# A small product moved from the end of a three-block kernel to the two ends of its recurrence

## The chip, the cores and the metric

The kernel runs on one core of a Trainium2 chip. The time is that of one execution on the device, in microseconds (us), from the first to the last instruction with what lies around it; less is better. The engines are TensorE (PE in the profile; PEld is its weight load), VectorE (DVE), ScalarE (ACT), GpSimd (POOL) and SyncE (SP). Each takes its instructions from a queue of its own, in the order in which the program was built; ACTq, POOLq and SPq are the transfers that an engine issues.

## What is computed

One sequence of 512 positions and 1024 channels passes through three blocks: the first of attention, gating and two feed-forward networks, the second a recurrent block with a convolution branch, the third with a chunked recurrence, differential attention, a convolutional feed-forward network and, at its very end, this:

```python
x = x + (jax.nn.gelu(gt) * val) @ w_down[l]

hg = rmsnorm(x, norm_ple_g[l])
x = x + jax.nn.sigmoid(hg @ w_ple_gate[l]) * (p[l].astype(x.dtype) @ w_ple[l])

return rmsnorm(x, norm_final_g)
```

`p` is an input of 512 x 256 and `w_ple` one of 256 x 1024. Their product depends on nothing that the three blocks compute.

## The kernel before

Activations lie with channels on the 128 partitions and the 512 positions along them, so x is eight tiles of 128 x 512, the chunks. Every product in float32 is made of three matmuls in a rounded 32-bit format: both factors are split into a high part and the rest, and `mm3` (L121 to L126) adds high by high (L123), rest by high (L124) and high by rest (L125). Weights come in slabs through `wsplit` (L100 to L119): SyncE's queue loads `raw` (two buffers), ScalarE casts it to `whi`, VectorE or GpSimd subtracts to get `wlo`, by the turn that the running number `n_slab` has in a list. `split` does the same for an activation: a cast on ScalarE (L194), a subtraction on VectorE (L195). Its results are called `hid..`, `phi`/`plo` (for p) or `hhi`/`hlo` (for a normed x). `gemm_fm` runs a product in groups of up to four output chunks, each in one PSUM bank of four that are called `psg`.

A scheduler lays the instructions out when the program is built: of those whose inputs are known it takes the one of highest priority, and a piece traced under `high_priority(offset=...)` has its priority moved by that offset. The product of p runs at −250, that is, below what is traced around it. Buffers come from pools; one pool named "tmp" of three buffers serves the transposed p (`pT`), the squares of norms (`sqn`) and other short-lived tiles.

The stretches that matter here, with the times at which the profiled execution reaches them:

- The **first seam**, at 1309: the last feed-forward product of block 1 (`ffn_swiglu(1)`, w_down) ends, `double_norm` squares the chunks of x (ScalarE, L808), adds the squares up with and without a gain (VectorE, L812 and L813), sums over channels on TensorE (`ps_sum`, L817), goes through a chain of small VectorE operations (`rs_v` to `diag`) and spreads the result with two matmuls (`ps_bc`, L272). Then the first product of block 2 starts on `hhi`.
- The **recurrence**, from about 1350 to 2060: 64 steps of a chain of small matmuls (`ps_y`, `ps_u`, `ps_s`) between which matmuls of other work are laid.
- The **second seam**, at 2111: block 2's output product ends, a norm follows (squares `sq` and, for the last chunk, `sql`; sums L235; `rs_v`, `ps_bc`), then the feed-forward network `ffn_relu2`.
- At 2890, ahead of block 3's feed-forward network, `ple_in` loads p by ScalarE's queue (L1696), transposes it on TensorE (L1701), copies it from PSUM (L1703) and splits it.
- At 3255, behind that network, `ple` makes the product with w_ple, 48 matmuls, whose results ScalarE copies from PSUM to `pl` (L1712), and then the gate product.

Of the kernel before, what the change touches and what calls it, by code (L numbers as in the profile page):

```python
# [9 lines left out]
F32 = mybir.dt.float32  # L10
# [6 lines left out]
T = 512  # L17
# [301 lines left out]
def fm_groups(c0, n, per=4, last=()):  # L319

    out, m = [], 0
    sizes = [per] * ((n - sum(last)) // per) + list(last)
    for k in sizes:
        out.append(([(c0 + m * 128, k * 128)], [(m + i, i * 128, 128) for i in range(k)]))
        m += k
    return out
# [1053 lines left out]
class Block3:  # L1380
# [323 lines left out]
            pact.append(self.split(t, c, pp, "p"))  # L1704
        return pact

    def ple(self, pp, pact):
        nc, a = self.nc, self.a
        pl = [pp.tile([128, T], F32, name=f"pl{c}") for c in range(8)]

        def ev_p(m, ps):
            nc.scalar.copy(pl[m], ps)  # L1712
        self.gemm_fm(a["w_ple_3"][0], 0, pact, fm_groups(0, 8), ev_p)
        act, y, R = self.norm_in(("norm_ple_g_3", 0))

        def ev_g(m, ps):
            t = self.tmp("pg")
            nc.vector.tensor_tensor(out=t, in0=ps, in1=R, op=ALU.mult)
            nc.scalar.activation(out=t, in_=t, func=AF.Sigmoid)
            (nc.vector if m > 5 else nc.gpsimd).tensor_tensor(out=t, in0=t, in1=pl[m], op=ALU.mult)  # L1720
            nc.vector.tensor_tensor(out=self.x[m], in0=self.x[m], in1=t, op=ALU.add)
        self.gemm_fm(a["w_ple_gate_3"][0], 0, act, fm_groups(0, 8, last=LAST), ev_g)
# [99 lines left out]
class Net(Prog, Block1, Block2, Block3):  # L1822
# [12 lines left out]
    def run(self, out):  # L1835
        usual = {"s": 2, "t": 1, "o": 1}
        with ExitStack() as st:
            self.psum_phase(st, usual, {})
            self.load_x(self.a["x"][0])
            self.par("A", PAR_A)  # L1840
            self.layer0()
            self.ffn_swiglu(0, extra=self.ada)
            self.par("B", PAR_B)
            self.layer1()
            self.ffn_swiglu(1)
            y12, y1 = self.double_norm("final_gain", 1e-6, 1e-6)
            act = self.block2_in(self.bcast(y12, sb=False))
        self.block2(act, y1)
        with ExitStack() as st:
            self.psum_phase(st, usual, {})  # L1850
            self.par("C", PAR_C)
            self.ffn_relu2()
            self.block3_mix()
            pp = st.enter_context(self.tc.tile_pool(name="ple", bufs=1))
            pact = self.ple_in(pp)
            self.ffn_conv()
            self.ple(pp, pact)
            self.finish(out)


# [17 lines left out]
```

## Time and profile before

| what | value |
|---|---|
| median of three runs | 3339.99 us (3333.66 to 3345.63) |
| profiled execution, its own time | 3332.78 us |
| its span, first to last instruction | 3331.0 us |
| TensorE busy | 3179.2 us, 95% |
| VectorE, ScalarE, GpSimd busy | 2041.3, 1386.5 and 515.1 us |
| mean granted TensorE clock | 0.983 |

Busy shares are averages over stages with different limits. A granted clock of 1 is TensorE's upper level (2.4 GHz), 0.5 the lower (1.2 GHz).

### The profile page before, as it was taken

How to read it: one execution, taken by the hardware profiler on the slowest of the kernel's cores; microseconds unless marked ns; L12 is line 12 of the kernel's file. 1: busy time of each engine (PE TensorE's matmuls, PEld its weight loads, DVE VectorE, ACT ScalarE, POOL GpSimd, SP SyncE). 2: the span in 40 equal slices, each digit the busy share in tenths (PEclk: the TensorE clock that was granted, in tenths of full speed). 3: DMA queues.
4: the chain of work that ended last, by engine and by line, in shares of the span. 5: the costliest groups of instructions: out<-in, count | busy, mean ns of one | idle time of the engine just before them, and what ended most of it. 6: DMA issues, size and time to landing. Idle time of an engine off the chain costs nothing. (4 is left out here: it accounts for less than half of the span.)

```text
span 3331.0 us, 43197 instructions
## 1 busy us (share of the span) xinstructions
PE 3179.2 (95%) x15337; PEld 2471.1 (74%) x15337; DVE 2041.3 (61%) x4002; ACT 1386.5 (42%) x2784; POOL 515.1 (15%) x603
## 2 busy tenths in 40 slices
PE   8999999999999999898899889999999999999998
PEld 6755778788778887666666656788877777788887
DVE  4576764654665356688778875434367764575665
ACT  3466332333443233454444444433244553343444
POOL 1000010111211011222223323111010011110111
PEclk9999999999999999999999999999999999999999
DMA  4411553525223332322122343233233125332322
GB/s 134 120 62 50 172 169 128 176 97 149 68 83 95 100 97 76 103 63 68 52 68 66 101 134 113 85 96 95 95 92 112 55 84 164 110 95 95 95 95 82
DMA packets 275032, 332.60 MB, mean 100 GB/s; under 512 B 52956, under 2 KB 188058, under 8 KB 274817
## 3 DMA queue, kind: packets, MB, share of 16 engines
q1 hardware_dynamic: 237392, 301.43, 29.4%
q10 hardware_dynamic: 33489, 12.39, 1.5%
q0 software_dynamic: 3936, 16.03, 1.5%
q8 instruction: 121, 1.98, 0.2%
q14 instruction: 94, 0.77, 0.1%
HBM read 311.88 MB, written 23.89 MB: 101 GB/s over the span
## 5 line engine op out<-in xcount | busy, mean ns | idle before, releaser
L118 DVE TENSOR_TENSOR wlo<-raw,whi 128x512 fp32r<-128x512 f32 (+2 forms) x865 | 625.2, 734 | 752.7 <-PE psg L124 419.3
L123 PE MATMUL psg<-hhi,whi 128*128 128x512 f32 (+1 forms) x2624 | 1044.5, 401 | 36.4 <-DVE glu L1301 7.0
L125 PE MATMUL psg<-hhi,wlo 128*128 128x512 f32 (+1 forms) x2624 | 1038.9, 397 | 13.3 <-DVE wlo L118 7.9
L124 PE MATMUL psg<-hlo,whi 128*128 128x512 f32 (+1 forms) x2624 | 1041.2, 397 | 0.0
L117 ACT CAST whi<-raw 128x512 fp32r<-128x512 f32 (+2 forms) x975 | 581.7, 604 | 1072.6 <-PE psg L124 924.6
L123 PEld LDWEIGHTS psg<-hhi,whi 128*128 128x128 f32 (+1 forms) x2624 | 496.5, 189 | 162.8 <-issue 17.2
L125 PEld LDWEIGHTS psg<-hhi,wlo 128*128 128x128 f32 (+1 forms) x2624 | 496.7, 189 | 124.9 <-POOL wlo L118 9.6
L124 PEld LDWEIGHTS psg<-hlo,whi 128*128 128x128 f32 (+1 forms) x2624 | 497.1, 189 | 107.2 <-issue 7.6
L123 PE MATMUL psg<-hidhi,whi 128*128 128x512 f32 x784 | 308.4, 394 | 1.0 <-DVE ffu L574 0.8
L125 PE MATMUL psg<-hidhi,wlo 128*128 128x512 f32 x784 | 308.0, 393 | 0.0
L124 PE MATMUL psg<-hidlo,whi 128*128 128x512 f32 x784 | 305.9, 390 | 0.0
L1305 DVE SCALAR_TENSOR_TENSOR z<-glu,par_B,z 128x512 f32<-128x512 f32 x240 | 197.0, 835 | 1.5
L118 POOL TENSOR_TENSOR wlo<-raw,whi 128x512 fp32r<-128x512 f32 (+1 forms) x110 | 146.8, 1341 | 281.3 <-ACT whi L117 217.3
L125 PEld LDWEIGHTS psg<-hidhi,wlo 128*128 128x128 f32 x784 | 147.2, 188 | 34.0
L124 PEld LDWEIGHTS psg<-hidlo,whi 128*128 128x128 f32 x784 | 147.2, 188 | 33.4
L123 PEld LDWEIGHTS psg<-hidhi,whi 128*128 128x128 f32 x784 | 147.4, 188 | 32.8 <-DVE ffu L574 1.3
L581 POOL TENSOR_TENSOR ffu<-ffu,ffg 128x512 f32<-128x512 f32 x44 | 64.7, 1469 | 582.6 <-DVE ffu L574 582.6
L1374 POOL TENSOR_TENSOR ffr<-ffr 128x512 f32<-128x512 f32 x32 | 40.1, 1261 | 293.0 <-ACT ffr L1373 286.9
L194 ACT CAST hidhi<-ffu 128x512 fp32r<-128x512 f32 x66 | 41.0, 622 | 106.1 <-POOL ffu L581 66.2
L195 DVE TENSOR_TENSOR hidlo<-ffu,hidhi 128x512 fp32r<-128x512 f32 x66 | 57.3, 868 | 30.9 <-ACT hidhi L194 29.4
L765 DVE SCALAR_TENSOR_TENSOR adacc<-adraw,c_act,adacc 128x1024 f32<-128x1024 f32 x42 | 53.9, 1284 | 33.4 <-DMA adraw<-in_ada_w_dram 33.0
L209 POOL TENSOR_TENSOR ss<-ss,sq 128x512 f32<-128x512 f32 x24 | 35.2, 1467 | 218.1 <-ACT sq L208 202.0
(572 smaller groups left out, 4040.3 us busy)
## 6 DMA issues: line engine op xcount, KB each, us to landing
raw<-in_ffn_w_gu_dram SPq DMA_DIRECT2D x176, 256.0 KB
raw<-in_w_in_dram SPq DMA_DIRECT2D x59, 512.0 KB
adraw<-in_ada_w_dram SPq DMA_DIRECT2D x48, 512.0 KB
raw<-in_w_up_dram SPq DMA_DIRECT2D x88, 256.0 KB
raw<-in_ffn_w_down_dram SPq DMA_DIRECT2D x42, 512.0 KB
raw<-in_w_ff_in_dram SPq DMA_DIRECT2D x32, 512.0 KB
raw<-in_w_ff_out_dram SPq DMA_DIRECT2D x32, 512.0 KB
raw<-in_w_in_dram SPq DMA_DIRECT2D x96, 128.0 KB
```

The costliest lines, as they stand in the source:

```text
L117: nc.scalar.copy(oi(hi), ri(r))
L118: eng.tensor_tensor(out=oi(lo), in0=ri(r), in1=fr(oi(hi)), op=ALU.subtract)
L123: first = nc.tensor.matmul(ps, lhsT=whi, rhs=xhi, start=start, stop=False)
L124: nc.tensor.matmul(ps, lhsT=whi, rhs=xlo, start=False, stop=False)
L125: nc.tensor.matmul(ps, lhsT=wlo, rhs=xhi, start=False, stop=stop)
L194: nc.scalar.copy(hi, t)
L195: nc.vector.tensor_tensor(out=lo, in0=t, in1=fr(hi), op=ALU.subtract)
L209: (nc.gpsimd if c < 4 else nc.vector).tensor_tensor(out=ss, in0=ss, in1=sq, op=ALU.add)
L581: nc.gpsimd.tensor_tensor(out=t, in0=t, in1=part[c], op=ALU.mult)
L765: nc.vector.scalar_tensor_tensor(out=acc, in0=raw, scalar=c[:, k:k + 1], in1=acc, op0=ALU.mult, op1=ALU.add)
L1305: tap = nc.vector.scalar_tensor_tensor(out=z[i], in0=g[:, j:j + T], scalar=cw(j), in1=z[i], op0=ALU.mult, op1=ALU.add)
L1374: nc.gpsimd.tensor_tensor(out=t, in0=t, in1=t, op=ALU.mult)
```

## The change

`ple_in` and the product with w_ple are called twice, once for each half of the output chunks, as `ple_half(g)` with priority −250: half 0 at the first seam, between `ffn_swiglu(1)` and `double_norm`, half 1 at the second, ahead of `ffn_relu2`. Each half loads and transposes p anew, makes 24 matmuls, copies four chunks from PSUM (L1715; the copies are named `plo` too, like the low part of p) and writes them to DRAM by GpSimd's queue (L1716). At the end `ple` loads the eight chunks again, by ScalarE's queue.

```diff
-    def ple(self, pp, pact):
+    def ple_half(self, g):
+
+        nc, a = self.nc, self.a
+        with self.tc.high_priority(offset=-250), self.tc.tile_pool(name=f"ple{g}", bufs=1) as pp:
+            pact = self.ple_in(pp)
+
+            def ev(m, ps):
+                t = pp.tile([128, T], F32, name=f"plo{m}")
+                nc.scalar.copy(t, ps)
+                nc.gpsimd.dma_start(out=self.pl_d[m], in_=t)
+            self.gemm_fm(a["w_ple_3"][0], 0, pact, fm_groups(0, 8)[g:g + 1], ev)
+
+    def ple(self, pp):
         nc, a = self.nc, self.a
         pl = [pp.tile([128, T], F32, name=f"pl{c}") for c in range(8)]
-
-        def ev_p(m, ps):
-            nc.scalar.copy(pl[m], ps)
-        self.gemm_fm(a["w_ple_3"][0], 0, pact, fm_groups(0, 8), ev_p)
+        for c in range(8):
+            nc.scalar.dma_start(out=pl[c], in_=self.pl_d[c])
...
             self.ffn_swiglu(1)
+            self.pl_d = self.tc.dram_tile([8, 128, T], F32, name="dram_ple")
+            self.ple_half(0)
             y12, y1 = self.double_norm("final_gain", 1e-6, 1e-6)
...
             self.par("C", PAR_C)
+            self.ple_half(1)
             self.ffn_relu2()
             self.block3_mix()
             pp = st.enter_context(self.tc.tile_pool(name="ple", bufs=1))
-            pact = self.ple_in(pp)
             self.ffn_conv()
-            self.ple(pp, pact)
+            self.ple(pp)
```

What this does to the order of the instructions is seen at the two seams. First ScalarE's queue at the first seam, before: the squares of x_75 to x_80 stand among the casts of w_down's last slabs.

```order
L808 ACTIVATE sqn<-x_75 128x512
L117 CAST whi<-raw 128x512
L808 ACTIVATE sqn<-x_76 128x512
L117 CAST whi<-raw 128x512 x4
L808 ACTIVATE sqn<-x_77 128x512
L117 CAST whi<-raw 128x512
L808 ACTIVATE sqn<-x_78 128x512
L117 CAST whi<-raw 128x512 x4
L808 ACTIVATE sqn<-x_79 128x512
L117 CAST whi<-raw 128x512
L883 DMA tri<-in_k_tri_dram 128x128
L808 ACTIVATE sqn<-x_80 128x512
```

The same place of the changed kernel:

```order
L117 CAST whi<-raw 128x512 x12
L1696 DMA p_10679<-in_p_dram 128x4x256
L194 CAST phi_10688<-pT 128x512
L808 ACTIVATE sqn<-x_74 128x512
L194 CAST phi_10699<-pT 128x512
L808 ACTIVATE sqn<-x_75 128x512
L808 ACTIVATE sqn<-x_76 128x512
L808 ACTIVATE sqn<-x_77 128x512
L117 CAST whi<-raw 128x512
L808 ACTIVATE sqn<-x_78 128x512
L808 ACTIVATE sqn<-x_79 128x512
L808 ACTIVATE sqn<-x_80 128x512
```

The twelve casts now come first, and all seven squares stand behind the load of p, six of them behind the second cast of p or next to it. In the changed program the load of p waits for TensorE's last w_down matmul; `tri` is loaded later, behind the first three `hhi`, and waits for the four writes of L1716.

VectorE's queue at the same place of the changed kernel, from the residual add of the last chunk (L300) on:

```order
L300 TENSOR_TENSOR x_80<-x_80,psg 128x512
L118 TENSOR_TENSOR wlo<-raw,whi 128x512
L1703 COPY pT<-ps_p 128x512 x2
L195 TENSOR_TENSOR plo_10689<-pT,phi_10688 128x512
L812 TENSOR_TENSOR s_10762<-s_10762,sqn 128x512
L813 SCALAR_TENSOR_TENSOR s_10763<-sqn,g_10754,s_10763 128x512
...
L812 TENSOR_TENSOR s_10762<-s_10762,sqn 128x512
L813 SCALAR_TENSOR_TENSOR s_10763<-sqn,g_10754,s_10763 128x512
L195 TENSOR_TENSOR plo_10700<-pT,phi_10699 128x512
L821 TENSOR_SCALAR rs_v_10804<-ps_sum_10761 128x8
```

Between the first `plo` and the second stand six pairs of L812 and L813 (two shown) and one `wlo`; before, one pair stood behind the residual add of x_80. TensorE has the 8 transposes behind the last w_down matmul, then 16 matmuls of p, the sums L817, the other 8 matmuls of p, and the two broadcasts `ps_bc`.

TensorE at the second seam, before:

```order
L235 MATMUL ps_sum<-one_z,ss 128x8
L235 MATMUL ps_sum<-ones,ss 128x2 x3
L124 MATMUL psg<-hlo_17067,whi 128x512
L125 MATMUL psg<-hhi_17066,wlo 128x512
L235 MATMUL ps_sum<-ones,sql 128x2 x4
L272 MATMUL ps_bc<-diag,ones 128x512 x2
L123 MATMUL psg<-hhi_17990,whi 128x512 x4
```

And in the changed kernel:

```order
L125 MATMUL psg<-hhi_17145,wlo 128x512
L1701 MATMUL ps_p<-ident,p_18009 128x128 x8
L235 MATMUL ps_sum<-one_z,ss 128x8
L235 MATMUL ps_sum<-ones,ss 128x2 x3
L235 MATMUL ps_sum<-ones,sql 128x2 x4
L123 MATMUL psg<-phi_18018,whi 128x512 x3
L124 MATMUL psg<-plo_18019,whi 128x512
...
L124 MATMUL psg<-plo_18030,whi 128x512
L272 MATMUL ps_bc<-diag,ones 128x512
```

The transposes of p now stand ahead of all sums of the norm, and 17 matmuls of p between the sums and the first broadcast; one lies between the broadcasts and six behind them. On VectorE the two copies `pT` stand ahead of `rs_v`, and the two `plo` behind the first and the third operation of the chain. On ScalarE the load of p stands behind `sql`.

Between the seams the lists differ on every engine: the two extra slabs shift the turns by which `wlo` goes to VectorE or GpSimd, and matmuls that are laid between the steps of the recurrence change places. At the end, w_ple's two loads are gone from SyncE's queue, and each seam has one.

## Rows read from the trace of the kernel before

**Rows 1.** The page, part 1: busy time by engine, share of the span, instructions.

```profile
PE 3179.2 (95%) x15337; PEld 2471.1 (74%) x15337; DVE 2041.3 (61%) x4002; ACT 1386.5 (42%) x2784; POOL 515.1 (15%) x603
```

**Rows 2.** Windows: length, busy us by engine, granted clock, DMA share, GB/s.

```profile
1300.00:1320.00 20.00, 13.30 (x67) 11.18 (x65) 13.46 (x32) 3.96 (x7) 9.09 (x26) 0.83 0.29 84
2100.00:2120.00 20.00, 13.95 (x64) 10.58 (x62) 10.91 (x28) 4.73 (x8) 0.19 (x1) 0.88 0.27 79
1350.00:2060.00 710.00, 627.61 (x3851) 455.12 (x3850) 550.78 (x1179) 338.16 (x859) 201.63 (x233) 0.95 0.29 82
```

**Rows 3.** Timeline of TensorE at the end: start, us, engine, line, operation.

```profile
3255.66 0.40 PE L123 MATMUL psg<-phi,whi 128*128 128x512 f32 x1
...
3266.43 0.39 PE L125 MATMUL psg<-phi,wlo 128*128 128x512 f32 x1
3266.66 0.28 PE L235 MATMUL ps_sum<-one_z,ss 128*128 128x8 f32 x2
```

**Rows 4.** Groups of TensorE, 3255.5 to 3267: busy us and mean ns, idle before.

```profile
L123 PE MATMUL psg<-phi,whi 128*128 128x512 f32 x16 | 6.3, 394 | 0.0
```

**Rows 5.** Timeline around the transposes of p; idle time and its releaser in brackets.

```profile
2890.09 0.40 ACTq L1696 DMA_DIRECT2D p<-in_p_dram  x1
...
2894.23 1.07 PE L1701 MATMUL ps_p<-ident,p 128*128 128x128 f32 x8 [0.29 <-issue]
2894.90 1.29 DVE L1703 COPY pT<-ps_p 128x512 f32<-128x512 f32 x2 [1.65 <-PE ps_p L1701]
...
2895.05 0.47 PE L125 MATMUL psg<-hhi,wlo 128*128 128x512 f32 x1
...
2895.62 0.62 ACT L194 CAST phi<-pT 128x512 fp32r<-128x512 f32 x1 [3.56 <-DVE pT L1703]
```

**Rows 6.** Timeline of the first seam.

```profile
1309.08 0.40 PE L125 MATMUL psg<-hidhi,wlo 128*128 128x512 f32 x1
...
1310.72 0.68 DVE L812 TENSOR_TENSOR s<-s,sqn 128x512 f32<-128x512 f32 x1
...
1311.33 0.74 DVE L813 SCALAR_TENSOR_TENSOR s<-sqn,g,s 128x512 f32<-128x512 f32 x1
...
1311.46 1.99 PE L817 MATMUL ps_sum<-sel,s 128*128 128x8 f32 x16 [1.98 <-DVE s L812]
...
1319.88 1.40 PE L272 MATMUL ps_bc<-diag,ones 128*128 128x512 f32 x2 [4.72 <-DVE diag L270]
...
1322.87 1.22 PE L123 MATMUL psg<-hhi,whi 128*128 128x512 f32 x2 [1.59 <-ACT hhi L785]
...
1325.12 0.63 PE L123 MATMUL psg<-hhi,whi 128*128 128x512 f32 x1
...
1326.82 0.43 PE L124 MATMUL psg<-hlo,whi 128*128 128x512 f32 x1
```

**Rows 7.** Timeline of the second seam.

```profile
2111.13 0.40 PE L125 MATMUL psg<-hhi,wlo 128*128 128x512 f32 x1
...
2112.34 0.63 ACT L224 ACTIVATE sql<-xr 128x512 f32<-128x512 f32 x1 [0.35 <-DVE xr L909]
...
2113.03 1.05 PE L235 MATMUL ps_sum<-ones,sql 128*128 128x2 f32 x8 [1.51 <-ACT sql L224]
2114.12 0.16 DVE L283 TENSOR_SCALAR rs_v<-ps_sum 128x4 f32<-128x4 f32 x1 [1.21 <-PE ps_sum L235]
...
2117.31 1.40 PE L272 MATMUL ps_bc<-diag,ones 128*128 128x512 f32 x2 [3.23 <-DVE diag L270]
...
2120.30 1.22 PE L123 MATMUL psg<-hhi,whi 128*128 128x512 f32 x2 [1.59 <-ACT hhi L785]
...
2125.59 0.41 PE L124 MATMUL psg<-hlo,whi 128*128 128x512 f32 x1
```

**Rows 8.** Waits of TensorE, 1350 to 2060: total us, times, longest.

```profile
PE ps_u L1255 <- ACT zV L1252: 18.6, 7, 5.9
```

**Rows 9.** Transfers of the whole run: count, KB each, median us from issue to landing.

```profile
dram_gates<-gs POOLq DMA_DIRECT2D x16, 256.0 KB, 2.6
```

## Prediction

> **What bounds the kernel now.** I read the page first: TensorE is busy for 95% of the span [rows 1], so a matmul that disappears where TensorE never stops gives back its whole time, and one added where TensorE waits anyway may cost nothing. Which of the two a place is must be read stage by stage, so I went to the timeline at the four places that the diff touches.
>
> At the end of the run the 48 matmuls of p with w_ple (three groups of 16, one of which is in [rows 4]) follow without a gap: the first starts at 3255.66, the last at 3266.43, and the sums of the norm behind them at 3266.66 [rows 3]. TensorE waits for nothing here, so this is 11.0 us of plain work at 0.23 us each.
>
> At the first seam TensorE does almost nothing between the end of the last w_down matmul, 1309.08 + 0.40 = 1309.48, and the first hhi matmul of block 2 at 1322.87: 13.4 us, in which the sums of the double norm, a chain of small VectorE operations and two broadcasts follow one another [rows 6]. At the second seam the gap goes from 2111.53 to 2120.30, 8.8 us [rows 7]. The granted clock is 0.83 and 0.88 in the two stretches [rows 2], and the first matmuls behind each seam take 0.63 us, until one of 0.43 at 1326.82 and of 0.41 at 2125.59 [rows 6, 7]: the lower level, 1.2 GHz, then 2.4. Between the seams TensorE is busy 627.6 of 710 us [rows 2]. So there is idle time in each seam for 24 matmuls (5.5 us at 0.23, 10 at twice that). But a seam is a chain, and what counts is whether an added operation stands in front of a link of it.
>
> **The change, part by part.** *The end.* All 48 matmuls leave a stretch without gaps, and the norm and the gate product move up: −11.0. The eight copies from PSUM leave ScalarE too; the eight loads that replace them wait for nothing late and have the whole gate product until their first use. The gate product then starts behind the adds of the last two chunks of x, but its order takes these chunks last; I take nothing for it.
>
> *The transposes of p at 2894.* They go. TensorE waited 0.29 us for its queue, worked on them until 2895.05, so 2895.05 − 2894.23 + 0.29: −1.1 [rows 5].
>
> *First seam.* The order of the built program decides it (shown with the change). The load of p stands on ScalarE's queue behind all casts of w_down, and it waits for the last w_down matmul, since p's buffer lies in memory that the feed-forward's pool held until then. Count from T0 = 1309.48. In the old place the transposes began 4.14 us after the load's issue (2890.09 to 2894.23), the copy pT 0.67 later, both copies took 1.29, and phi began 0.72 after pT [rows 5]. So the transposes come at T0+4.1, pT at T0+4.8 to 6.1, phi at about 5.5 to 6.2. Now for what is queued behind: on ScalarE the seven sqn squares of x_74 to x_80 stand behind phi, where six of them ran under the w_down product before; on VectorE six of the pairs of adds L812/L813 that consume them stand behind pT and the first plo. Before, only the last pair ran after T0 (1310.72 and 1311.33, 0.61 apart [rows 6]). Now plo ends at about T0+6.8 (one VectorE operation of this size, 0.68 [rows 6]), then twelve adds at 0.61 and a wlo among them at 0.6 take 7.9: the last pair ends at T0+14.7, its L812 starts at 13.5 in place of 1.24. The sums, the chain and the broadcasts follow as before, so the first hhi matmul slips by the same: **+12.3**. The 16 matmuls of the product that stand ahead of the sums end in time (from T0+6.8, 16 at twice 0.23 is 7.4, to T0+14.2, when the last add that the sums need is at 14.2 as well), the eight behind the sums lie under the VectorE chain, which took from 1311.46 to 1319.88 with the sums [rows 6]. So the work is hidden, and its preparation isn't. Bounds: +8.2 if the load took no time, +15 if the adds also wait for the three buffers that pT and the squares share.
>
> *Second seam.* Here p's load waits for no matmul, but stands behind the last square sql, issued at 2112.34 [rows 7]. With 4.14 the transposes come at 2116.5 and take 1.07 [rows 5]. The order puts them ahead of the sums of the norm, both the early ones and the last: 16 small matmuls, 2.1 us by twice the 1.05 of eight [rows 7]. So rs_v starts at 2119.7 in place of 2114.12. Two plo operations were put between the links of the chain behind it, 1.2; the rest, 2114.12 to 2117.31, is 3.2. The broadcast comes at 2124.1 in place of 2117.31: +6.8. Of the matmuls put ahead of it, 14 need plo (from 2120.3): 3.2 us at 0.23, 6 at double, so in the first case they fit, in the second they add 2. For that, TensorE then comes to the hhi matmuls out of a stretch of work, and part of the 5.3 us at the lower level (2120.30 to 2125.59), half of which would be saved, comes back. I take 1.0 off: **+5.8**, bounds +3.9 and +9.
>
> A rule of the Trainium skill bears on both seams. The row has 4.14 us from the issue of 512 KB to the transposes [rows 5]. The page "DMA: Bandwidth & Descriptors" (section "Anatomy of one DMA — SWDGE (gpsimd) path") gives a fixed cost of about 2.0 us plus the bytes at 436 GB/s; an estimate from that page is 3.2 us, and with it each seam would be 0.9 shorter and the sum 1.8 lower. The sum goes by the row.
>
> *The recurrence.* The low priority lets no product matmul drift into it, but it is ordered anew on every engine: the split of w_ple takes two of the slab numbers by which wlo goes to VectorE or GpSimd, and the lists shift. Its longest wait of TensorE is ps_u for zV, 18.6 us in seven waits [rows 8]. I take 0, and half of those 18.6 either way as the bound: ±9.
>
> Sum: −11.0 − 1.1 + 12.3 + 5.8 = **+6.0**. On the profiled execution, 3332.78 (span 3331.0 and 1.8 around it), that is 3338.8. That execution is 7.2 below the median of the runs shown, 3339.99, so the forecast for a median is 3346. A difference under 0.3%, 10 us, is about what a measurement here can't tell from no change.
>
> **The rivals.** *The seams hide it all.* If the load of p does not hold up the squares and adds (it lands early, or the adds run under the product after all), 11.0 + 1.1 are simply gained: 3328. For it speaks the idle time of 13.4 and 8.8 us, against it the queue order, in which the squares are behind phi. With the added matmuls TensorE could also stay at 2.4 GHz: of the 3.95 us from 1322.87 to 1326.82 and the 5.3 at the second seam half, 4.6, less the 1.0 I have counted; then 3324. The Trainium skill, "TensorE: Matmul & The Clock Gate" (section "Why this matters for your kernels"), advises against idle gaps between bursts of matmuls for this reason; the two stretches of lower clock behind the seams agree.
>
> *Slower: the writes of plo hold ScalarE up.* At the first seam four writes of 256 KB go out from GpSimd's queue to DRAM, and the load of tri on ScalarE, placed behind the first three hhi, waits for them to land, with five hhi behind it that TensorE needs. The copies end at about T0+22.5, and a write of this size lands in 2.6 [rows 9], so 25.1; ScalarE comes to tri at about T0+27. There are 2 us to spare. From a landing of 4.6 on every microsecond is added; at 9 it is +4.4, together +10.4, 3350. GpSimd's memsets wait for the same writes.
>
> *The recurrence's new order* gives 3337 or 3355 at its bounds, and decides the sign together with the seams.
>
> **How the numbers follow.** The forecast, the seams' delay about cancelled by the end, within 0.3%: 0.47. Its own range is 3336 to 3350. The seams hide it: 0.09, and a recurrence that saves 16 or more, beyond its bound: 0.06. Faster is 0.15. The writes: 0.15; a seam at its upper bound (+3 each) or a recurrence at its: 0.23. Slower is 0.38. The range adds to 3346 the bounds of the recurrence (±9) and of the seams (−6, +6): 3331 to 3361; I widen it downward to 3328, the case that hides all.
>
> **What would show it.** Right, if p's load at the first seam is issued at the end of the w_down product, six pairs L812/L813 run after it, the first hhi matmul comes about 26 us after the last w_down matmul (13.4 before) and about 15.6 at the second seam (8.8 before), and the gate product follows w_down directly. Wrong, if the pairs run under the product, if tri is issued late with hhi behind it, or if TensorE's idle time between the seams moves by more than 9 us from 82.

## The result and the profile after

The changed kernel takes 3382.23 us (median of four, 3380.91 to 3383.75), the kernel before 3340.29 beside it: a ratio of 1.0129, 95% interval 1.0113 to 1.0145. That is 42 us slower; the forecast was 3346, range 3328 to 3361. The two profiled executions lie 51.0 apart in span, since that of before (3332.78) lies 7.5 below its median and that of after (3383.75) 1.5 above.

Where the 51 went is told by six marks of TensorE's timeline in both traces. The first seam is the gap between the last w_down matmul and the first hhi matmul behind it, the stretch between the seams runs from there to the last matmul of block 2's output product, and so on:

| stage, us | before | after | difference |
|---|---|---|---|
| start to the last w_down matmul of block 1 | 1309.5 | 1313.2 | +3.7 |
| first seam | 13.4 | 28.4 | +15.0 |
| between the seams | 788.7 | 822.5 | +33.9 |
| second seam | 8.8 | 18.7 | +9.9 |
| to the last w_down matmul of block 3 | 1135.5 | 1133.3 | −2.2 |
| from there to the start of TensorE's last row | 64.4 | 54.8 | −9.6 |

TensorE does the same work in the first stage of both kernels, and in the experiments below that leave this work as it is the stage takes 1309.1 to 1315.4: its 3.7 is within the spread between executions. The largest part of the loss is the stretch between the seams.

Part 1 of the page hardly moves against [rows 1]: TensorE is busy 20.8 us more in a span 51 longer.

```profile
PE 3200.0 (95%) x15345; PEld 2488.6 (74%) x15345; DVE 2046.9 (61%) x4006; ACT 1388.1 (41%) x2786; POOL 521.1 (15%) x611
```

The first seam in the timeline of after, to be read beside [rows 6] (the rows of several engines, in order of time):

```profile
1312.82 0.40 PE L125 MATMUL psg<-hidhi,wlo 128*128 128x512 f32 x1
1313.25 0.37 ACTq L1696 DMA_DIRECT2D p<-in_p_dram  x1
...
1317.21 1.06 PE L1701 MATMUL ps_p<-ident,p 128*128 128x128 f32 x8 [4.00 <-DMA p<-in_p_dram]
1317.88 1.29 DVE L1703 COPY pT<-ps_p 128x512 f32<-128x512 f32 x2 [3.33 <-PE ps_p L1701]
...
1319.86 0.68 DVE L812 TENSOR_TENSOR s<-s,sqn 128x512 f32<-128x512 f32 x1
1320.46 0.74 DVE L813 SCALAR_TENSOR_TENSOR s<-sqn,g,s 128x512 f32<-128x512 f32 x1
...
1326.09 0.69 DVE L118 TENSOR_TENSOR wlo<-raw,whi 128x512 fp32r<-128x512 f32 x1 [2.35 <-ACT whi L117]
...
1329.23 0.68 DVE L812 TENSOR_TENSOR s<-s,sqn 128x512 f32<-128x512 f32 x1
...
1330.06 3.54 PE L817 MATMUL ps_sum<-sel,s 128*128 128x8 f32 x16 [4.19 <-DVE s L812]
...
1341.65 0.88 PE L123 MATMUL psg<-hhi,whi 128*128 128x512 f32 x2 [1.59 <-ACT hhi L785]
```

The load is issued as the w_down product ends, the transposes wait 4.0 us for it, and the six pairs of adds run from 1319.86 to 1330.6. The last L812 begins at 1329.23, 16.0 us after the product's end in place of 1.24. One link was not foreseen: the wlo among the pairs waits 2.35 us for a cast that itself waits for TensorE's matmuls of p, which run at the lower clock (0.63 us each). The 24 sums behind the adds then run at the lower clock too, 5.2 us in place of 3.7, but the chain from `rs_v` to the broadcast takes 3.6 in place of 4.7.

The second seam of after, beside [rows 7]:

```profile
2163.78 0.39 PE L125 MATMUL psg<-hhi,wlo 128*128 128x512 f32 x1
...
2165.00 0.40 ACTq L1696 DMA_DIRECT2D p<-in_p_dram  x1
2168.99 1.94 PE L1701 MATMUL ps_p<-ident,p 128*128 128x128 f32 x8 [4.82 <-DMA p<-in_p_dram]
...
2172.59 1.85 PE L235 MATMUL ps_sum<-ones,sql 128*128 128x2 f32 x8
...
2174.47 0.16 DVE L283 TENSOR_SCALAR rs_v<-ps_sum 128x4 f32<-128x4 f32 x1 [2.81 <-PE ps_sum L235]
...
2177.95 0.68 DVE L270 TENSOR_TENSOR diag<-ident,bc_h 128x512 fp32r<-128x512 f32 x1
...
2180.18 0.39 PE L272 MATMUL ps_bc<-diag,ones 128*128 128x512 f32 x1
...
2182.88 0.97 PE L123 MATMUL psg<-hhi,whi 128*128 128x512 f32 x3 [0.45 <-ACT hhi L785]
```

Here the load is 3.99 us old when the transposes start, as taken. But behind 4.8 us of waiting TensorE has fallen to its lower level (granted clock 0.50 from 2169.00 to 2174.50): eight transposes take 1.94 in place of 1.07 [rows 5], eight sums 1.85 in place of 1.05 [rows 7]. The first `diag` is ready at 2178.63, and its broadcast starts only at 2180.18, behind the matmuls of p that stand ahead of it. In return the hhi matmuls start at the upper level, 0.97 for three, where before two took 1.22.

At the end the gate product follows w_down at 0.23 us, as forecast; before, these two rows were 12.03 us apart. The first two lines are of before, the others of after:

```profile
3255.43 0.39 PE L125 MATMUL psg<-hidhi,wlo 128*128 128x512 f32 x1
...
3267.46 0.48 PE L123 MATMUL psg<-hhi,whi 128*128 128x512 f32 x1
```

```profile
3315.76 0.39 PE L125 MATMUL psg<-hidhi,wlo 128*128 128x512 f32 x1
3315.99 0.39 PE L123 MATMUL psg<-hhi,whi 128*128 128x512 f32 x1
```

Between the seams, the windows of the two kernels (length, busy us by engine, granted clock), before and after:

```profile
1322.87:2111.53 788.66, 705.04 (x4185) 516.77 (x4185) 594.53 (x1253) 371.47 (x914) 225.01 (x255) 0.95 0.29 85
```

```profile
1341.65:2164.17 822.52, 711.39 (x4177) 522.74 (x4177) 601.05 (x1255) 371.66 (x914) 236.90 (x281) 0.94 0.28 82
```

TensorE is idle 111.1 us in place of 83.6, and its work takes 6 us more at a lower mean clock. The waits of TensorE in that stretch of after:

```profile
PE ps_yt L1281 <- ACT Y L1278: 21.9, 9, 7.7
PE ps_v L1248 <- DVE S L1261: 12.7, 5, 6.4
PE psg L123 <- ACT glu L1298: 12.1, 3, 6.6
PE psg L125 <- DVE wlo L118: 9.0, 2, 5.2
PE ps_u L1255 <- ACT zV L1252: 8.4, 4, 4.1
```

The wait on which the forecast's bound was built fell from 18.6 [rows 8] to 8.4, and three others grew that the forecast didn't look at. The first two of them before:

```profile
PE ps_yt L1281 <- ACT Y L1278: 3.4, 2, 1.8
PE ps_v L1248 <- DVE S L1261: 1.7, 2, 1.0
```

The third, the product for ScalarE's glu, was 0.6. It isn't one wait that grew, but another order with other holes.

### The profile page after: what moved, and what is told of

It reads as the page before. It is cut to its first block, busy times and chain, and to the rows that moved or that the text cites. A ratio compares the mean times of both kernels' runs of the same rounds, so it can differ in the third digit from the quotient of the medians.

```text
span 3382.0 us, 43287 instructions
## 1 busy us (share of the span) xinstructions
PE 3200.0 (95%) x15345; PEld 2488.6 (74%) x15345; DVE 2046.9 (61%) x4006; ACT 1388.1 (41%) x2786; POOL 521.1 (15%) x611
## 5 line engine op out<-in xcount | busy, mean ns | idle before, releaser
L118 DVE TENSOR_TENSOR wlo<-raw,whi 128x512 fp32r<-128x512 f32 (+1 forms) x865 | 624.0, 733 | 761.2 <-PE psg L124 408.7
```

Of the source, the lines that this page charges most:

```text
L118: eng.tensor_tensor(out=oi(lo), in0=ri(r), in1=fr(oi(hi)), op=ALU.subtract)
```

## The experiments

Two theories stood. A: the 34 us between the seams come from the two slab numbers that w_ple's split takes, which shift the turn of VectorE and GpSimd, and with it the order that the scheduler builds. B: they are the first seam's lateness carried on (the writes of plo, the load of tri, GpSimd's memsets behind them).

**The turn alone, and the change without it.** The first kernel is the one before with this line at the first seam, the second the changed one with its reverse behind the first half:

```diff
+            self.n_slab += 2
             y12, y1 = self.double_norm("final_gain", 1e-6, 1e-6)
```

```diff
             self.ple_half(0)
+            self.n_slab -= 2
             y12, y1 = self.double_norm("final_gain", 1e-6, 1e-6)
```

> The kernel before, with nothing of the change but its two slab numbers: n_slab is raised by 2 at the first seam, so that from there on the turn of VectorE and GpSimd for wlo is the changed kernel's. In the built program TensorE's order through the recurrence is then word for word that of the changed kernel. Theory A (the recurrence's 36 us come from that turn and the order that follows from it): +36 on the kernel before, about 3376, with the shift all between the seams. Rival B (they come from what runs late out of the first seam: the load of tri behind the four writes, GpSimd's memsets): no change, 3340.

> The changed kernel with n_slab lowered by 2 behind the first half, so that the recurrence is built in the order of before, while both seams, the writes and the end stay as changed. Theory A: the recurrence's 36 us are gone and the rest stays, first seam +15, second +5, end -10: about +10, 3350. Rival B: the seam's lateness is still there, so about 3382 as changed.

The turn alone: 3371.57 against 3337.10, ratio 1.010 (1.0084 to 1.0117), and its stretch between the seams is as long as that of after, longer even, at a granted clock of 0.92 (the profiled execution took 3381.65, 10 us above the median):

```profile
1327.48:2159.32 831.84, 724.16 (x4185) 533.06 (x4185) 599.15 (x1253) 372.04 (x914) 224.16 (x255) 0.92 0.28 80
```

Its waits are those of after (ps_yt for Y 22.7, ps_v for S 13.7). The change without the turn: 3348.09, ratio 1.0029 (1.0018 to 1.0040), the stretch at 790.7 again and ps_u for zV at 18.8:

```profile
1340.88:2131.59 790.71, 705.88 (x4177) 515.84 (x4177) 595.62 (x1255) 371.81 (x914) 233.76 (x281) 0.95 0.30 86
```

A holds both ways. B falls, since the second kernel has the late seam, the writes and the late load of tri, and its stretch behind them is only 2.0 us longer than before; other kernels with the order of before show 785.7 to 793.1 there.

**Is the order of before a lucky one?** Three more turns: raised by 1 at the first seam; the changed turn in the first half of the recurrence only; in the second half only. The line of the last one, in the loop over the eight pairs of heads:

```diff
+                if p == 4:
+                    self.n_slab += 2
                 low["y7"] = self.rwkv_steps(P, y_d)
```

> The kernel before with n_slab raised by 1 at the first seam: the third turn that the list of three has. Its order through the recurrence is a third one. Theory A1 (the order of before is a lucky one among several, any other costs tens of us): 3360 to 3385. Theory A2 (the turn raised by 2 is an unlucky one): within 10 us of 3340.

> The kernel before with the changed turn of slabs in the first half of the recurrence only: n_slab is raised by 2 at the first seam and by 1 more at pair 4 of 8, which gives the turn of before again. Up to step 24 TensorE's order is the changed kernel's. If the loss is made in the second half by the turn there: about 3340. If it is made by what the first half puts off (690 product matmuls ahead of step 24 in place of 761 by the built orders), it stays: 3360 to 3372.

> The kernel before with the changed turn of slabs from pair 4 of 8 of the recurrence on: n_slab is raised by 2 there. TensorE's order is that of before up to step 24. If the loss belongs to the second half under the changed turn: 3355 or more. If it belongs to the first half (raising the turn in the first half alone cost 24): within 10 of 3337.

| turn raised by, first half and second | time beside before | between the seams |
|---|---|---|
| 0, 0 (before) | | 788.7 |
| 2, 2 | 1.0100 (1.0084 to 1.0117) | 831.8 |
| 1, 1 | 1.0049 (1.0034 to 1.0064) | 809.7 |
| 2, 0 | 1.0070 (1.0055 to 1.0085) | 816.6 |
| 0, 2 | 1.0035 (1.0022 to 1.0049) | 803.6 |

All four are slower, by 12 to 34 us. The stretches are those of the profiled executions, which lie 10.1, 0.4, 6.4 and 1.9 us above their medians, in the order of the table. Raised by 1 lies between its two readings. The first half alone keeps 24 of the 34, as the second reading of its expectation had it; but the second half alone costs 12 as well, which neither of its readings had: the loss sits in no one place. Nor is it all idle time. In the last kernel TensorE is idle 87.6 us between the seams, where before it was 83.6, but busy 716.0 in place of 705.0 with the same 4185 matmuls, at a lower mean clock:

```profile
1327.44:2131.04 803.60, 715.99 (x4185) 525.41 (x4185) 595.63 (x1253) 374.31 (x914) 226.93 (x255) 0.94 0.28 83
```

These times don't tell what makes the loss: that VectorE and GpSimd make other slabs, or that the fillers stand elsewhere. A kernel for the second part: two neighbouring pieces of filler work change places, and n_slab is set so that every slab keeps its engine.

```diff
-            order = ["c01", "c12", "c31 g02", "c42", "g22", "c62 g41", "g51 h01", "g62 h13 n h44 x p y04 n2 q r y43 m08 s", "x yw y7 w"]
+            order = ["c01", "c12", "c31 g02", "c42", "g22", "g41 c62", "g51 h01", "g62 h13 n h44 x p y04 n2 q r y43 m08 s", "x yw y7 w"]
...
                 for f in order[p + 1].split():
+                    self.n_slab += {"g41": 8, "c62": -10}.get(f, 0)
                     filler(f)
+                    self.n_slab += {"c62": 2}.get(f, 0)
```

> The kernel before with two neighbouring pieces of filler work in the second half of the recurrence traced in the other order (c62 and g41), and with every slab keeping the engine that it had: the number of wlo on VectorE and on GpSimd is the same for each size, and TensorE's order is that of before up to step 30 of 64 and another one behind it. If the order of the fillers by itself is worth 10 us and more: 3347 or more, the recurrence's stretch longer by 10 or more. If what costs is only which engine makes which wlo: 3337 within 5.

Measured: 3346.54 against 3336.79, ratio 1.0034 (1.0021 to 1.0046), so 7 to 15 us. The order by itself is worth some 10 us. Where they sit isn't shown: the profiled execution took 3338.42, 8 us below that median, and its 793.8 between the seams is hardly more than kernels with the order of before show. What share the order has of the 34 isn't shown either.

**What the first seam's 15 us are.** From here on all kernels keep the turn of before. One loads, transposes and splits p ahead of block 1's last feed-forward network, in a pool of its own; one keeps the late load and traces the half behind the double norm:

```diff
+            pe = st.enter_context(self.tc.tile_pool(name="pe", bufs=1))
+            early = self.ple_in(pe)
             self.ffn_swiglu(1)
...
-            self.ple_half(0)
+            self.ple_half(0, early)
+            self.n_slab -= 2
             y12, y1 = self.double_norm("final_gain", 1e-6, 1e-6)
```

```diff
-            self.ple_half(0)
             y12, y1 = self.double_norm("final_gain", 1e-6, 1e-6)
+            self.ple_half(0)
+            self.n_slab -= 2
```

> The changed kernel with the order of the recurrence kept as before (n_slab lowered by 2), and with p for the first seam loaded, transposed and split ahead of the last feed-forward network of block 1, in a pool of its own; the 24 matmuls stay in the seam, the second half stays as changed. Measured so far with the late p: 3348. If the first seam's +15 is the late load and the squares and adds queued behind it, the squares run under the w_down product again, the transposes cost 1 there, the matmuls ahead of the sums 1 to 3: 3348 - 15 + 3 = 3336. Rival: the 24 matmuls themselves, at the lower clock, hold the seam up: 3342 or more.

> The changed kernel with the order of the recurrence kept as before, and the first half traced behind the double norm and not ahead of it. The squares and the adds then run under the w_down product as before; p's load still waits for the last w_down matmul, and its transposes and 13 matmuls stand between the sums and the broadcast. If the queue behind the squares is the first seam's cost, most of the +15 is gone and some +5 for the matmuls at the lower clock come in: 3348 - 15 + 5 = 3338. If the late load by itself is the cost: 3348 as it was.

Early p: 3333.86, ratio 0.9989 (0.9981 to 0.9998). The gap of the seam is 13.0 (13.2 and 13.8 in two later kernels with the same edit), about the 13.4 of before, with all 24 matmuls in it:

```profile
1314.41 0.39 PE L125 MATMUL psg<-hidhi,wlo 128*128 128x512 f32 x1
1314.64 0.39 PE L123 MATMUL psg<-phi,whi 128*128 128x512 f32 x1
...
1316.93 0.97 PE L817 MATMUL ps_sum<-sel,s 128*128 128x8 f32 x8
...
1322.63 0.40 PE L125 MATMUL psg<-phi,wlo 128*128 128x512 f32 x1
1324.43 0.50 PE L272 MATMUL ps_bc<-diag,ones 128*128 128x512 f32 x1 [1.40 <-DVE diag L270]
...
1327.77 1.22 PE L123 MATMUL psg<-hhi,whi 128*128 128x512 f32 x2 [1.60 <-ACT hhi L785]
```

The matmuls lengthen the gap by no more than 0.4: they follow w_down without a pause, stay at the upper level (0.39), and the sums between them take 0.97 for eight, the rate of before [rows 6], where after had 3.54 for 16. Only the last wait, for hhi, brings the lower level back. With the norm first: 3336.89, ratio 1.0006 (0.9996 to 1.0015), a gap of 15.4. Here the load is as late as in the changed kernel, so its lateness and the matmuls of p together cost 2 of the 15 us. The other 13 are what the changed kernel queued behind the load: the squares on ScalarE and the adds on VectorE. The product itself isn't the cost.

**The second seam.** Both halves there, none at the first; then, on top of the early p, the second half traced behind the norm:

```diff
-            self.ple_half(0)
...
             self.par("C", PAR_C)
+            self.ple_half(0)
             self.ple_half(1)
```

```diff
         y, R = self.rstd(self.sumsq(self.x), 1024, 1e-6, sb=False)
+        self.ple_half(1)
         A = self.sp.tile([128, 8], F32, name="ada_Af", bufs=1)
...
-            self.ple_half(1)
             self.ffn_relu2()
```

> Both halves at the second seam, none at the first; the recurrence keeps the order of before and the first seam is untouched. If the second seam costs what the changed kernel's trace shows (+5) and the other half's p is split under the first's, the other 24 matmuls add at most their own 5.5: 3340 - 10 + 5 + 0 to 7 = 3335 to 3342. If each half pays its own load of p behind the sums: 3340 - 10 + 10 + 5 = 3345 or more.

> The kernel with the early p at the first seam and the order of the recurrence kept, and in addition the second half traced behind the norm of the second seam: the sums then stand ahead of the transposes of p, these behind the first broadcast, and 13 matmuls of p ahead of the first hhi matmul. With the second half ahead of the norm the gap of the second seam was 18.9 in place of 8.8. If the wait of the sums for p's load is that cost, the broadcast comes as before and the hhi matmul waits for the matmuls of p alone: a gap of 10 to 14, in all 3334 - 5 to - 8 = 3326 to 3329. If the matmuls of p are the cost, the gap stays near 19 and the time at 3334.

Both halves: 3355.26, ratio 1.0054 (1.0039 to 1.0069), the rival reading and worse: the gap is 40.3 us, and each half waits for its own load of p (in brackets TensorE's idle time ahead of the row).

```profile
2120.16 1.94 PE L1701 MATMUL ps_p<-ident,p 128*128 128x128 f32 x8 [4.98 <-DMA p<-in_p_dram]
...
2141.86 1.94 PE L1701 MATMUL ps_p<-ident,p 128*128 128x128 f32 x8 [11.49 <-DMA p<-in_p_dram]
```

Norm first: 3332.09, ratio 0.9983 (0.9974 to 0.9992), with the sums and the broadcast as early as before and a gap of 12.9, as expected. The time that was expected with it, 3326 to 3329, is missed. The rows of TensorE:

```profile
2118.92 0.40 PE L125 MATMUL psg<-hhi,wlo 128*128 128x512 f32 x1
2120.82 1.05 PE L235 MATMUL ps_sum<-ones,sql 128*128 128x2 f32 x8 [1.50 <-ACT sql L224]
2125.11 0.79 PE L272 MATMUL ps_bc<-diag,ones 128*128 128x512 f32 x1 [3.23 <-DVE diag L270]
...
2132.26 0.40 PE L123 MATMUL psg<-hhi,whi 128*128 128x512 f32 x1
```

Beside the early p alone the time fell less than the gap, 2 to 3 us against 6, and the two intervals overlap: the 11 matmuls of p that are left stand among the hhi matmuls, and the stage behind takes 1136.0 in place of 1132.0. It is the fastest version tried, beside the next one, and 6 us ahead of the kernel before.

**Half of it.** The first half at the first seam with the early p, the second left at the end, with `ple_in` at 2890 as before:

```diff
-            self.ple_half(1)
...
+            pact = self.ple_in(pp)
             self.ffn_conv()
-            self.ple(pp)
+            self.ple(pp, pact)
```

> Only the first half moves, to the first seam, with its p loaded early as in the early kernel; the second half's 24 matmuls stay at the end with the transposes at 2890, and the second seam is as before. The end gives back half, -5.5; the early transposes cost 1, the first seam 1 to 3: 3337 - 5.5 + 3 = about 3334. Rival (24 matmuls cost their time in the seam, too): 3337 to 3342.

Measured 3332.36, ratio 0.9987 (0.9978 to 0.9996), first seam 13.8 (the matmuls of p behind the sums run at a granted clock of 0.53 here, 1317.00 to 1320.00), end 59.7 in place of 64.4: moving half of the product is worth 1 to 7 us, and the 5.5 that it took at the end lie within that. The move of the other half adds nothing that can be measured (0.9983 with it, 0.9987 without, and the intervals overlap).

## Why the prediction was wrong, step by step

*The recurrence is the step that failed.* The prediction saw the cause (two slab numbers, the turn of wlo, a new order) and priced it at "I take 0, and half of those 18.6 either way as the bound: ±9". It measured +34 with the turn alone. The bound was drawn from the largest wait of the old order. Here the new order didn't lengthen that wait, it made others (ps_yt, ps_v, glu), and the busy time moved with the clock. The idle time of the stretch rose from 83.6 to 111.1, which is what the prediction itself had named as a sign of being wrong. Nor was zero the middle: of five other orders measured none was faster than that of before.

*The first seam*, mechanism right, size short: +12.3, measured +15.0. The missing part is mostly the 2.35 us that the wlo among the adds waits for its cast; the slower sums and the faster chain behind them nearly cancel. It is at the bound of 15 that was given for another reason, the shared buffers.

*The second seam*: forecast +5.8, measured a gap of +9.9, of which about 1 comes back in the stage behind (−2.2 there, 1.1 of it the transposes at 2890). The load and its place were right; the transposes and sums were priced at the upper clock and ran at the lower, 0.9 and some 1.5 us dearer. The rest is mostly the broadcast's place behind the matmuls of p, which the prediction had named for up to 2 and put at nothing in its sum.

*The end*: −11.0 forecast; the matmuls gave 11.8 between w_down and the gate product, and 2.2 went back in the rows behind, −9.6. *The transposes at 2890* lie inside the −2.2.

So without the recurrence the sum was +6.0 and the kernel without the turn measured +10 (0.0018 to 0.0040 of 3337, 6 to 13 us): right in sign and kind, short by some 4 us, in the one wait, the clock and the broadcast's place.

*The rivals.* That a seam hides the product came true at the first seam alone, and only when p was loaded early: the gap is then 13.0 to 13.8, 13.4 before. The rival's second part, that the added matmuls keep TensorE at its upper level, did not come true with it: the first two hhi matmuls behind the early product take 1.22, as before, and the granted clock is 0.52 from 1327.70 to 1333.00. This part came true at the second seam of the changed kernel (0.97 for three), whose gap was longer all the same. In the changed kernel the rival was wrong, as the queue order said. By the advice of the Trainium skill quoted there ("TensorE: Matmul & The Clock Gate", "Why this matters for your kernels") the idle time ahead of the transposes should cost clock. At the second seam the rows agree: behind 4.8 us of it eight transposes took 1.94 in place of 1.07. At the first they don't, or not at once: behind 4.0 us eight took 1.06 at a granted clock of 0.95, and most of the matmuls of p behind them ran at 0.50. The 3.2 us for the load that the prediction estimated from the Trainium skill ("DMA: Bandwidth & Descriptors", "Anatomy of one DMA — SWDGE (gpsimd) path") rest on a fit for transfers that GpSimd issues, and p's load goes by ScalarE's queue: the transposes came 3.96 and 3.99 us after the issue, near the 4.14 of the row. The writes of plo did hold up what the prediction named, at little cost:

```profile
1340.88 2.04 ACT L785 ACTIVATE hhi<-h,mod 128x512 fp32r<-128x512 f32 x3 [0.68 <-DVE h L784]
...
1344.06 2.06 DVE L784 SCALAR_TENSOR_TENSOR h<-x,ada_A,ps_bc 128x512 f32<-128x512 f32 x3
...
1344.44 0.35 ACTq L883 DMA_DIRECT2D tri<-in_k_tri_dram  x1
...
1345.80 0.49 ACTq L1046 DMA_DIRECT2D WD<-in_w_decay_up_dram  x1
1346.33 0.72 ACT L785 ACTIVATE hhi<-h,mod 128x512 fp32r<-128x512 f32 x1 [3.42 <-DVE h L784]
```

The load of tri goes out 1.5 us after the third hhi ends, with three more loads behind it. The fourth hhi starts behind these, at 1346.33, though the h that it needs, the first of three from 1344.06 at 0.74 us each, was ready at 1344.80: this rival's chain is there, and it delays ScalarE by 1.5 us. TensorE shows no wait for it at this place. From the first hhi matmul to the first step of the recurrence (the first VU copy) it is 104.6 us in the changed kernel, 107.0 in the one without the turn, 105.2 before, so by these traces what runs late here costs 2 us at most.

## What to carry to other kernels

Work put into a gap is free only if its inputs are there when the gap begins: here 24 matmuls were free as soon as their load, transposes and split had been done earlier, and 15 us dear when these stood in front of the gap's own chain on two in-order queues. Before an edit is priced, look for counters and turns that it shifts for code far behind it; hold them fixed, or measure the shift alone, since a new order of such a loop can cost more than the edit (34 us here, the rest of the change 10). And the largest wait of the old order is no bound for a reordered stretch: five other orders cost 10 to 34 us where the largest wait was 18.6, by new waits and by a lower clock.

## What the runs showed that was not expected

Two neighbouring fillers exchanged, with every slab on the same engine, cost 10 us of 3337 (1.0021 to 1.0046). Through the stretch between the seams the same 4185 matmuls were busy 705.0 us in the order of before and 724.2 with the turn raised by 2, at mean granted clocks of 0.95 and 0.92: the order with the longer idle time (107.7 us against 83.6) also had the lower clock. That the one brings the other isn't shown: with the turn raised in the second half only, idle time was 87.6 and the matmuls were busy 716.0 all the same. And eight 128 x 128 transposes took 1.94 us behind 4.8 us of idle TensorE at the second seam, but 1.06 behind 4.0 at the first, and 1.07 behind 0.29 [rows 5].
